# Six changes of order in a two-layer hybrid encoder on one core: low parts, turned pairs, dot products and the sums of its branches

## The chip, the cores and the metric

The kernel runs on one core of one Trainium2 chip. A core has five engines that run at the same time, each through its own queue in order: TensorE (PE, matrix products; its weight loads are PEld), VectorE (DVE), ScalarE (ACT), GpSimd (POOL) and SyncE (SP, which issues DMA transfers). The metric is the device time of one execution in microseconds (us). The time before is 2328.27 us, the median of three runs (2327.64 to 2328.99).

## The reference

The inputs are x (512 tokens by 1024 channels) and one conditioning row c. Each of two layers adds a half-step feed-forward, a mixer of three branches, and another half-step feed-forward; each takes a normed x, scaled and shifted from c:

```python
mod = (c_act @ w_ada[l] + b_ada[l]).reshape(B, N_MOD, D_MODEL)          # nine rows of 1024
h = modulate(rms_norm(x, norm_gain[l, 0]), mod[:, 0], mod[:, 1])
x = x + 0.5 * mod[:, 2][:, None, :] * swiglu(h, ffn_w_gate[l, 0], ffn_w_up[l, 0], ffn_w_down[l, 0])
h = modulate(rms_norm(x, norm_gain[l, 1]), mod[:, 3], mod[:, 4])
x = x + mod[:, 5][:, None, :] * hybrid_mixer(h, ...)
# hybrid_mixer:
proj = h @ w_in
qa, ka, va, ub, qc, kc, vc, f_lin, g_lin = jnp.split(proj, SPLIT_POINTS, axis=-1)
ya = chunked_relpos_attention(...)      # branch A: 8 heads of 64, learned bias by distance
yb = multiscale_pool(ub, ...)           # branch B: window averages of 2, 4, 8, 16 tokens, per group of 128
yc = forgetting_attention(...)          # branch C: causal, forget gates in the logits
branch = jnp.einsum('bsnw,nwd->bsnd', jnp.stack([ya, yb, yc], axis=2), w_branch)
merged = jnp.sum(jax.nn.sigmoid(g_lin.reshape(B, S, 3, D_MODEL)) * branch, axis=2)
return merged @ w_out
```

All is float32. Queries and keys of A and C are RMS-normed per head.

## The kernel before, in words

**Products.** An fp32 operand is cut in a rounded high part (fp32r) and a low part, the rest. A product is three matmuls: high by high, high by low, low by high. `triple` does that for 512 columns (L140 to L142), `add_product` for 256 (L149 to L151); both call `poll` first. High parts are casts on ScalarE (L317 for weights), low parts are subtractions on VectorE (L319), in the first phase on GpSimd. The long products with h (gate and up of the feed-forwards, the gates of the merge) go by a seven-product scheme on blocks: `Seven` makes the weights' sums and splits (L563 to L580, casts L567 and low parts L568), `Blocks` the sums and splits of h, beginning with `h`, which adds high and low part back to full blocks (L522).

**Phases of a layer.** Feed-forward, mixer, feed-forward. The first feed-forward begins with `start`: squares of x, their sum over channels by matmuls with ones (L829), 1/rms by three Newton steps on VectorE (L328 to L337), spread over the partitions by a matmul (L843), and then for each of eight blocks of 128 channels: the weights' chunk (its low part on GpSimd, L319), h scaled (L852), its high part (ScalarE, L854) and low part (VectorE, L857), and 18 matmuls.

The mixer: `proj_qk` and `proj_v` make queries, keys and values of A (columns 0, 1, 2). `proj` evacuates an accumulator per token block; for values that is a cast (L944) and a subtraction (L945) into the tile xv. Then follow attention A with the projections of C (columns 3, 4, 5) as filler between its steps, attention C with the first gate and branch A's merge as filler, the pooling inputs, two tiles of the merge of C (`merge_units`), and the merges by pairs of tiles (`merge_pairs`: three pairs of branch C, four of branch B), then w_out. In attention, L1108 and L1109 are logits, L1112 adds the bias and takes the maximum, L1116 is the exponential, L1120 the division, L1132 turns the probabilities, L1136 and L1137 split them (tiles pta and ptb), and L1154 and L1155 multiply by the values. In `merge_pairs` the sums of branches are `put_c`: gate times branch on VectorE (L1395), then added to the running sum on GpSimd (L1396). `put_b` calls it too, and splits an earlier sum (L1402, L1403).

**Queries and keys** are normed and scaled per token block (`scale`, L980), then turned, 128 channels (a pair of heads) at a time: `turn`, four transposes (L985), a high part on ScalarE (L994) and a low part on VectorE (L1000). There are four PSUM buffers for such results (`mmt`), four accumulators (`acc`), and two buffers of the kind ptb.

**Rows of w_ada.** The 144 blocks of modulation are dot products of VectorE (L227) with rows loaded by DMA (L220). `side_work`, called by each chunk of weights (`wchunk`), loads the next row and computes those loaded, as long as `in_ffn` is set; it is cleared behind the values of A. In the pairs rows are loaded and computed where `rows` is called.

**What sets the order.** `pe[0]` counts TensorE's work in matmuls of 512 columns. `later(delay, fn)` puts a step off until so much work has been issued, and `poll` runs what is due. Queries and keys are normed from such due times, and `ready` turns pair p when due, and not before attention has come to a given head (`heads`). `after` and `behind` put an instruction behind another one in the queue (`tc.issue_after`). The instructions are then laid in each engine's queue by a scheduler; each engine runs its queue in that order and waits on semaphores.

Of the kernel before, what the change touches and what calls it, by code (L numbers as in the profile page):

```python
# [15 lines left out]
F32 = mybir.dt.float32  # L16
# [3 lines left out]
ALU = mybir.AluOpType  # L20
# [20 lines left out]
def encoder_kernel(tc, xT, c, w_ada, b_ada, gains, w_gate, w_up, w_down, w_qkv, w_f, w_ubg,  # L41
# [457 lines left out]
    class Blocks:  # L499
# [18 lines left out]
        def h(self, q):  # L518
            if self.xa is None:
                self.full[q] = blk("v2", F32)  # L520
                k = slice(2 * q, 2 * q + 2)
                nc.vector.tensor_tensor(self.full[q], hhi[:, k, :].bitcast(F32), hlo[:, k, :].bitcast(F32), op=ALU.add)  # L522
# [182 lines left out]
    class Ffn:  # L705
# [112 lines left out]
        def start(self):  # L818
# [15 lines left out]
            r = rsqrt(v, NT)  # L834
            dg = st([P, NT, P], F32, "ssum", 1)
# [5 lines left out]
            spread = gate["vector"]  # L841
# [8 lines left out]
            def h(d):  # L850
                t = t1(T)
                scaled = nc.vector.tensor_tensor(t, rb, xd(d), op=ALU.mult).ins  # L852
                a, b = apre[:, l, 0, d:d + 1], modc[:, l, 0, d:d + 1]
                nc.scalar.activation(hhi[:, d, :], t, AF.Identity, scale=a, bias=b)  # L854
                tb = mmt()
                nc.scalar.activation(tb, t, AF.Identity, scale=a, bias=b)
                nc.vector.tensor_tensor(hlo[:, d, :], tb, hhi[:, d, :].bitcast(F32), op=ALU.subtract)  # L857
# [13 lines left out]
            for d in range(KD):  # L871
                if d == 0:
                    gate["vector"] = spread
# [10 lines left out]
    def qkv_chunk(l, col, c, **kw):  # L884
        return wchunk(w_qkv[l, 2 * c * P:(2 * c + 2) * P, col * T:(col + 1) * T]
                      .rearrange("(k p) c -> p k c", p=P), (2, T), **kw)

    def proj(l, col, evac, pre=None, norm=None):
# [25 lines left out]
        else:  # L914
            for c in range(2):
                if col == 3 and c == 1:
                    gate["vector"] = last["values"]
                hi, lo = qkv_chunk(l, col, c)
# [7 lines left out]
        for t in range(NT):  # L926
            for c, hi, lo in held:
# [8 lines left out]
    def proj_v(l, col, tag, res):  # L936
        vt = [None] * NT

        def evac(t, a):
            b = st([P, H, 2, HD], F32R, tag, 4)  # L940
            a3 = a.rearrange("p (h d) -> p h d", h=H)
            for odd in range(2):
                hi, lo = b[:, odd::2, odd, :], b[:, odd::2, 1 - odd, :]
                nc.scalar.copy(hi, a3[:, odd::2, :])  # L944
# [6 lines left out]
    def proj_qk(l, col, gcol, is_q, res, pre=None, norm=None):  # L951
# [30 lines left out]
        def turn(p):  # L982
# [7 lines left out]
            first, second = slice(0, HD), slice(HD, P)  # L990
            for odd, (own, other) in enumerate(((first, second), (second, first))):
# [288 lines left out]
    def merge_pairs(l, jobs, first, blocks):  # L1280
# [7 lines left out]
        for q, (n, d, ys, put, early, late, behind) in enumerate(jobs):  # L1288
# [38 lines left out]
            tens(c[:, 0], w, c[:, 0], ALU.add)  # L1327
            step("pair34")
# [20 lines left out]
    class Mixer:  # L1349
# [10 lines left out]
        def run(self, nxt):  # L1360
# [31 lines left out]
            def put_c(d, pb, th):  # L1392
# [3 lines left out]
                nc.gpsimd.tensor_tensor(md, md, tmp, op=ALU.add)  # L1396
# [41 lines left out]
            front(3)()  # L1438
            for n, _ in enumerate(merge_units(l, 2, yc, put_c, 2)):
                if n == 4:  # L1440
# [7 lines left out]
                elif n == 14:  # L1448
# [3 lines left out]
            jobs = [(2, 2, yc, put_c, [], [back(3), back(2)], [front(1)]),  # L1452
                    (2, 4, yc, put_c, [cast(1)], [back(1)], [front(0)]),
                    (2, 6, yc, put_c, [cast(0)], [back(0)], [])]
            def rows(*tags):
                def go():
                    mod_flush()
# [5 lines left out]
            def reload():  # L1463
                silc[0] = st([P, D], F32, "b", NB)
                nc.sync.dma_start(silc[0], sil_dram.broadcast_to([P, D]))
                rows("pta", "b")()

            jobs += [(1, d, yb, put_b, [] if d else [reload], [], [rows("pta") if d else rows("pta", "b")]) for d in (0, 2, 4, 6)]
# [93 lines left out]
```

## Time and profile before

| what | us |
|---|---|
| median of three runs | 2328.27 (2327.64 to 2328.99) |
| the profiled execution | 2328.61 |
| its span, first to last instruction | 2326.8 |
| TensorE busy | 2299.0 (99%) |
| VectorE busy | 1855.7 (80%) |
| ScalarE busy | 1240.8 (53%) |
| GpSimd busy | 333.1 (14%) |

TensorE's granted clock is 1.00. Spans and starts in the rows of the profile are microseconds from the first instruction. A row of the timeline is: start, duration, engine, line, operation, written tile <- read tiles, shape, count, and in brackets the engine's idle time before it and what ended it. A row of the list of waits is: the waiting engine and line, what released it, microseconds in total, times, the longest. A row of the windows has the stretch, its length, and the busy time of PE, PEld, DVE, ACT and POOL with their counts, the granted clock, the DMA share and GB/s. Matmuls are pipelined, so that a row's duration (0.39) is longer than the distance of two starts.

### The profile page before, as it was taken

To read this page: it belongs to the slowest core of one execution; us is meant where nothing else is said; L and a number is where in the kernel's file an instruction comes from. 1 tells how busy PE (TensorE), PEld (TensorE's weight loads), DVE (VectorE), ACT (ScalarE), POOL (GpSimd) and SP (SyncE) were. 2 spreads that over 40 slices of the span, in tenths; PEclk is the share of its full clock that TensorE was granted. 3 is DMA by queue.
4 is the path that set the end of the run, shared out by engine and by line. 5 is a ranking of instruction groups with operands and counts; after the bars stand their busy time and mean duration, and the time that the engine had idled before them with its cause. 6 is when DMAs were issued, how large, how long until landed. Compare 5 with 4: busy or idle time off the path is not lost.

```text
span 2326.8 us, 38930 instructions
## 1 busy us (share of the span) xinstructions
PE 2299.0 (99%) x14826; PEld 2067.4 (89%) x14826; DVE 1855.7 (80%) x3172; ACT 1240.8 (53%) x2252; POOL 333.1 (14%) x447
## 2 busy tenths in 40 slices
PE   7999999999999999999999999999999999999999
PEld 5899998778889898989999989988788898999898
DVE  8988877787698778888788989687877986879593
ACT  5353554677654464635553636466765544636362
POOL 3000011244412210000000000122443122000000
PEclk9999999999999999999999999999999999999999
DMA  8736343433234625363426373443333346153322
GB/s 283 252 110 225 120 162 122 120 91 118 96 118 135 204 71 203 101 248 115 145 82 208 91 254 100 163 145 101 94 118 94 118 145 199 55 181 96 114 92 100
DMA packets 142174, 325.26 MB, mean 140 GB/s; under 512 B 14338, under 2 KB 16514, under 8 KB 141988
## 3 DMA queue, kind: packets, MB, share of 16 engines
q1 hardware_dynamic: 137282, 307.05, 40.3%
q0 software_dynamic: 4704, 15.73, 2.2%
q8 instruction: 116, 1.90, 0.3%
q14 instruction: 70, 0.57, 0.1%
q10 hardware_dynamic: 2, 0.00, 0.0%
HBM read 312.16 MB, written 6.38 MB: 137 GB/s over the span
## 4 chain that ended last, share of the span: by engine, by line
PE 87%; DVE 8%; ACT 2%; issue 2%; DMA 1%; SPq 0%; DVEq 0%; ACTq 0%
PE acc L140 12%; PE acc L142 12%; PE acc L141 12%; PE acc L149 6%; PE acc L151 6%; PE acc L150 6%; PE mm L151 5%; PE mm L149 5%; PE mm L150 5%; PE mm L140 4%; PE mm L141 4%; PE mm L142 4%; PE mm L1132 1%; DVE v L227 1%; DVE w L319 1%
## 5 line engine op out<-in xcount | busy, mean ns | idle before, releaser
L317 ACT CAST w<-raw 128x1024 fp32r<-128x1024 f32 (+1 forms) x213 | 219.4, 1040 | 216.4 <-PE acc L142 132.7
L140 PE MATMUL acc<-b,w 128*128 128x512 f32 (+1 forms) x880 | 326.6, 371 | 0.0
L141 PE MATMUL acc<-b,w 128*128 128x512 f32 (+1 forms) x880 | 323.2, 367 | 0.0
L142 PE MATMUL acc<-b,w 128*128 128x512 f32 (+1 forms) x880 | 323.1, 367 | 0.0
L319 DVE TENSOR_TENSOR w<-raw,w 128x1024 fp32r<-128x1024 f32 x205 | 251.2, 1235 | 89.3 <-ACT w L317 85.8
L142 PEld LDWEIGHTS acc<-b,w 128*128 128x128 f32 x880 | 165.3, 188 | 28.1
L140 PEld LDWEIGHTS acc<-b,w 128*128 128x128 f32 x880 | 165.3, 188 | 26.3
L141 PEld LDWEIGHTS acc<-b,w 128*128 128x128 f32 x880 | 165.4, 188 | 25.9
L149 PE MATMUL acc<-b,ptb 128*128 128x256 f32 x588 | 162.9, 277 | 0.0
L150 PE MATMUL acc<-b,ptb 128*128 128x256 f32 x588 | 162.7, 277 | 0.0
L151 PE MATMUL acc<-b,ptb 128*128 128x256 f32 x588 | 162.6, 277 | 0.0
L227 DVE CUSTOM_DVE_ANT_0 v<-v,b,badac 128x1024 f32<-128x1024 f32 x108 | 142.1, 1328 | 5.2 <-DMA v<-in_w_ada_dram 5.2
L140 PE MATMUL acc<-w,hhi 128*128 128x512 f32 x336 | 138.5, 413 | 0.8 <-DVE xv L945 0.7
L141 PE MATMUL acc<-w,hhi 128*128 128x512 f32 x336 | 131.7, 392 | 0.0
L142 PE MATMUL acc<-w,hlo 128*128 128x512 f32 x336 | 131.4, 392 | 0.0
L568 DVE TENSOR_TENSOR ptb<-pta,ptb 128x1024 fp32r<-128x1024 f32 x70 | 85.7, 1224 | 50.9 <-ACT ptb L567 49.8
L149 PE MATMUL mm<-b,ptb 128*128 128x256 f32 x420 | 115.9, 276 | 0.0
L151 PE MATMUL mm<-b,ptb 128*128 128x256 f32 x420 | 115.9, 276 | 0.0
L150 PE MATMUL mm<-b,ptb 128*128 128x256 f32 x420 | 115.9, 276 | 0.0
L568 DVE TENSOR_TENSOR w<-v,w 128x1024 fp32r<-128x1024 f32 x84 | 102.5, 1220 | 16.1 <-ACT w L567 16.1
L478 DVE SCALAR_TENSOR_TENSOR xv<-acc,badac,xv 128x512 f32<-128x512 f32 (+1 forms) x112 | 76.9, 689 | 47.3 <-PE acc L142 47.2
L567 ACT CAST ptb<-raw 128x1024 fp32r<-128x1024 f32 x84 | 88.5, 1053 | 48.4 <-DVE raw L577 48.2
(330 smaller groups left out, 7401.3 us busy)
## 6 DMA issues: line engine op xcount, KB each, us to landing
v<-in_w_ada_dram SPq DMA_DIRECT2D x108, 512.0 KB, 5.5
raw<-in_w_down_dram SPq DMA_DIRECT2D x88, 512.0 KB, 4.2
raw<-in_w_qkv_dram SPq DMA_DIRECT2D x42, 512.0 KB, 3.7
v<-in_w_gate_dram SPq DMA_DIRECT2D x70, 256.0 KB, 4.3
v<-in_w_up_dram SPq DMA_DIRECT2D x70, 256.0 KB, 3.3
raw<-in_w_gate_dram SPq DMA_DIRECT2D x70, 256.0 KB, 3.5
raw<-in_w_up_dram SPq DMA_DIRECT2D x70, 256.0 KB, 3.5
raw<-in_w_ubg_dram SPq DMA_DIRECT2D x28, 512.0 KB, 3.6
```

What stands on the lines that cost most here:

```text
L140: mm(o, lh, rh, start=start, stop=False)
L141: mm(o, lh, rl, start=False, stop=False)
L142: mm(o, ll, rh, start=False, stop=stop)
L149: mm(o, lh, rh, start=start and k == 0, stop=False, skip_group_check=True)
L150: mm(o, lh, rl, start=False, stop=False, skip_group_check=True)
L151: mm(o, ll, rh, start=False, stop=k == 3, skip_group_check=True)
L227: product = lambda: nc.vector.tensor_tensor_reduce(out=raw, in0=raw, in1=silc[0], scale=1.0, scalar=badac[:, l, j, d:d + 1], op0=ALU.mult, ...
L317: nc.scalar.copy(hi, raw)
L319: lo_eng.tensor_tensor(lo, raw, hi.bitcast(F32), op=ALU.subtract)
L478: nc.vector.scalar_tensor_tensor(x, acc_j, gate, x, op0=ALU.mult, op1=ALU.add)
L567: act_(lambda: nc.scalar.copy(pair[0], src))
L568: vec_(lambda: nc.vector.tensor_tensor(pair[1], src, pair[0].bitcast(F32), op=ALU.subtract))
```

## The change

Six things change; no arithmetic does.

1. In `start`, the low part of the weights' first chunk on GpSimd is put behind a small new GpSimd operation (`paused`) that reads 1/rms; before it stood behind the sum of squares.
2. `Blocks.h` (L522 before) is put behind the last low part of h in `start`, as the dots already are where `last["norm"]` is set.
3. The first chunk of column 3 (queries of C) is loaded and split ahead of the last token block of column 2 (values of A), and the casts of its second chunk are put behind the last cast of the values.
4. A pair is turned only when 24 units have been issued since the turn before (`APART`), while attention runs, and keys are due 12 units later.
5. The sums of the pooling's widest window (`front(3)`) are issued behind the first matmuls of the merge of C instead of ahead of them.
6. In the pairs, the running sum is added on VectorE, and the dots of w_ada rows are spread: one at the end of a pair, one in its middle.

```diff
             if self.xa is None:
                 self.full[q] = blk("v2", F32)
                 k = slice(2 * q, 2 * q + 2)
-                nc.vector.tensor_tensor(self.full[q], hhi[:, k, :].bitcast(F32), hlo[:, k, :].bitcast(F32), op=ALU.add)
+                with after("norm"):
+                    nc.vector.tensor_tensor(self.full[q], hhi[:, k, :].bitcast(F32), hlo[:, k, :].bitcast(F32),
+                                            op=ALU.add)
...
             r = rsqrt(v, NT)
+            paused = nc.gpsimd.tensor_scalar(st([P, 16], F32, "hd", 1)[:, :NT], r, 1.0, None, op0=ALU.mult).ins
...
-            spread = gate["vector"]
...
-                nc.vector.tensor_tensor(hlo[:, d, :], tb, hhi[:, d, :].bitcast(F32), op=ALU.subtract)
+                low = nc.vector.tensor_tensor(hlo[:, d, :], tb, hhi[:, d, :].bitcast(F32), op=ALU.subtract)
+                if d == KD - 1:
+                    last["norm"] = low.ins
...
                 if d == 0:
-                    gate["vector"] = spread
+                    gate["vector"] = paused
                 w = wchunk(w_first[d], (6, P), side=False, lo_eng=nc.gpsimd)
...
+    ahead = []
...
                 if col == 3 and c == 1:
-                    gate["vector"] = last["values"]
-                hi, lo = qkv_chunk(l, col, c)
+                    gate["scalar"], gate["vector"] = last["values cast"], last["values"]
+                hi, lo = ahead.pop() if ahead else qkv_chunk(l, col, c)
...
         for t in range(NT):
+            if col == 2 and t == NT - 1:
+                ahead.append(qkv_chunk(l, 3, 0))
             for c, hi, lo in held:
...
+            turned[0] = pe[0]
             for odd, (own, other) in enumerate(((first, second), (second, first))):
...
-                if heads[0] < (Q_GATE if is_q else K_GATE)[p]:
+                if heads[0] < (Q_GATE if is_q else K_GATE)[p] or (heads[0] < H and pe[0] < turned[0] + APART):
                     later(8, lambda: ready(p))
...
-            later(TURN + 12 * p, lambda p=p: ready(p))
+            later(TURN + (0 if is_q else 12) + 12 * p, lambda p=p: ready(p))
...
-    TURN = 52
+    turned = [0.0]
+    TURN, APART = 52, 24
...
             tens(c[:, 0], w, c[:, 0], ALU.add)
+            for fn in middle:
+                fn()
             step("pair34")
...
                 vec_(lambda: nc.vector.scalar_tensor_tensor(tmp, th, 1.0, pb, op0=ALU.add, op1=ALU.mult))
-                nc.gpsimd.tensor_tensor(md, md, tmp, op=ALU.add)
+                vec_(lambda: nc.vector.tensor_tensor(md, md, tmp, op=ALU.add))
...
-            front(3)()
             for n, _ in enumerate(merge_units(l, 2, yc, put_c, 2)):
-                if n == 4:
+                if n == 0:
+                    front(3)()
+                elif n == 4:
...
-            jobs += [(1, d, yb, put_b, [] if d else [reload], [], [rows("pta") if d else rows("pta", "b")]) for d in (0, 2, 4, 6)]
+            jobs += [(1, 0, yb, put_b, [reload], [], [], [rows(2, "b", "pta")]),
+                     (1, 2, yb, put_b, [], [rows(1)], [], [rows(1, "pta")]),
+                     (1, 4, yb, put_b, [], [rows(1, "pta")], [], []),
+                     (1, 6, yb, put_b, [], [rows(1, "pta")], [], [])]
```

How the queues change is seen at three places. The line numbers of the changed kernel are larger by 2 to 12: L985 is L993 there, L1108 is L1118, L1132 is L1142, L1154 is L1164.

TensorE in attention A, layer 0, where the second pair of C's queries is turned (mm is a PSUM tile, ident,ptb a turn of queries, ident,t a turn of probabilities, acc<-w the projection that fills in). Before:

```order
L1108 MATMUL mm_5071<-b_4399,b_4145 128x512
L1109 MATMUL mm_5071<-b_4399,b_4146 128x512
L985 MATMUL mm_5083<-ident,ptb_4705 128x128 x4
L140 MATMUL acc_4859<-w_4997,hhi 128x512
L141 MATMUL acc_4859<-w_4997,hhi 128x512
L1132 MATMUL mm_5098<-ident,t_826_4986 128x128 x2
```

In the changed kernel, from the same logits on:

```order
L1118 MATMUL mm_5076<-b_4418,b_4147 128x512
L1119 MATMUL mm_5076<-b_4418,b_4148 128x512
L1142 MATMUL mm_5088<-ident,t_828_4991 128x128 x2
L140 MATMUL acc_4864<-w_5002,hhi 128x512
L141 MATMUL acc_4864<-w_5002,hhi 128x512
```

The turn L985 is gone from behind the logits; it now stands 23 rows further down the queue, with two groups of turned probabilities, a product by the values and another pair of logits in between.

VectorE behind the keys of A, layer 0 (nt_q, nt_u, nt_z are Newton steps, L980 scales the four token blocks of ptb, L319 is the low part of the last chunk of A's values). Before:

```order
L336 SCALAR_TENSOR_TENSOR nt_u_4300<-nt_q_4299,nt_v_633_4237 128x32
L337 SCALAR_TENSOR_TENSOR nt_z_4301<-nt_u_4300,nt_z_4259 128x32
L980 TENSOR_TENSOR ptb_4131<-ptb_4131,nt_z_4301 128x512 x2
L1052 TENSOR_SCALAR t_642_4272<-t_642_4272 8x512
L980 TENSOR_TENSOR ptb_4131<-ptb_4131,nt_z_4301 128x512 x2
L1054 SCALAR_TENSOR_TENSOR t_641_4269<-t_641_4269,t_642_4272 8x512
L319 TENSOR_TENSOR w_4391<-raw_4389,w_4391 128x1024
L1056 SCALAR_TENSOR_TENSOR t_643_4278<-t_641_4269 8x512
```

In the changed kernel (L988 is the scaling, L1062, L1064, L1066 and L1072 are L1052, L1054, L1056 and L1062 before):

```order
L227 ISA pta_4479,badac<-pta_4479,b_73,badac 128x1024
L227 ISA badac 128x1
L335 TENSOR_TENSOR nt_q_4301<-nt_z_4261 128x32
L336 SCALAR_TENSOR_TENSOR nt_u_4302<-nt_q_4301,nt_v_634_4239 128x32
L337 SCALAR_TENSOR_TENSOR nt_z_4303<-nt_u_4302,nt_z_4261 128x32
L1062 TENSOR_SCALAR t_643_4274<-t_643_4274 8x512
L988 TENSOR_TENSOR ptb_4133<-ptb_4133,nt_z_4303 128x512 x2
L1064 SCALAR_TENSOR_TENSOR t_642_4271<-t_642_4271,t_643_4274 8x512
L988 TENSOR_TENSOR ptb_4133<-ptb_4133,nt_z_4303 128x512
L1066 SCALAR_TENSOR_TENSOR t_644_4280<-t_642_4271 8x512
L988 TENSOR_TENSOR ptb_4133<-ptb_4133,nt_z_4303 128x512
L1072 TENSOR_SCALAR strip_4282<-t_644_4280 8x128
```

A dot product L227 (with the read of its sum) stands ahead of the last Newton step, the four scalings are spread over the forget gate's steps, and the low part L319, ahead of the scan before, comes behind the scan and the four strips L1072 now, four rows below the last one shown, with that of the next chunk behind it.

VectorE at the end of `start` (hlo is the low part of h, L522 the sum of a block). Before:

```order
L857 TENSOR_TENSOR hlo<-mm_395,hhi 128x512
L227 ISA v_75_401,badac<-v_75_401,b_73,badac 128x1024
L227 ISA badac 128x1
L522 TENSOR_TENSOR v_97_539<-hhi,hlo 128x1024
L227 ISA v_80_452,badac<-v_80_452,b_73,badac 128x1024
L227 ISA badac 128x1
L857 TENSOR_TENSOR hlo<-mm_431,hhi 128x512
```

In the changed kernel:

```order
L859 TENSOR_TENSOR hlo<-mm_397,hhi 128x512
L227 ISA v_76_403,badac<-v_76_403,b_73,badac 128x1024
L227 ISA badac 128x1
L859 TENSOR_TENSOR hlo<-mm_433,hhi 128x512
L227 ISA v_81_454,badac<-v_81_454,b_73,badac 128x1024
```

The block sum has left its place; between the last two low parts of h stands one dot.

More of the change, by code (lines that the diff above doesn't have):

```diff
@@ L943, in evac @@
                 hi, lo = b[:, odd::2, odd, :], b[:, odd::2, 1 - odd, :]
-                nc.scalar.copy(hi, a3[:, odd::2, :])
+                last["values cast"] = nc.scalar.copy(hi, a3[:, odd::2, :]).ins
                 last["values"] = nc.vector.tensor_tensor(lo, a3[:, odd::2, :], hi.bitcast(F32), op=ALU.subtract).ins
@@ L1287, in merge_pairs @@
         todo = [first, Seven(gates(*jobs[1][:2]), ENTRY, stag="v2")]
-        for q, (n, d, ys, put, early, late, behind) in enumerate(jobs):
+        for q, (n, d, ys, put, early, middle, late, behind) in enumerate(jobs):
             now = todo.pop(0)
@@ L1450, in run, with rows @@
             first.second()
[L1452 to L1455, printed above, removed]
+            jobs = [(2, 2, yc, put_c, [], [], [back(3), back(2)], [front(1)]),
+                    (2, 4, yc, put_c, [cast(1)], [], [back(1)], [front(0)]),
+                    (2, 6, yc, put_c, [cast(0)], [], [back(0)], [])]
+            def rows(dots, *tags):
                 def go():
-                    mod_flush()
+                    mod_flush(len(loaded) - dots)
                     for tag in tags:
```

2 lines of the change are left out of this document (1 added, 1 removed).

## The prediction

> **What bounds the kernel now.** I read the page first, then the list of TensorE's waits, then the timeline around each wait that the change touches.
>
> ```profile
> span 2326.8 us, 38930 instructions
> PE 2299.0 (99%) x14826; PEld 2067.4 (89%) x14826; DVE 1855.7 (80%) x3172; ACT 1240.8 (53%) x2252; POOL 333.1 (14%) x447
> ```
>
> TensorE is busy for 99% of the span and the change removes no matmul. Only what TensorE loses between matmuls can be won, and the list of waits says how much that is (line, what it waited for, sum in us, times, longest):
>
> ```profile
> PE mm L843 <- ACT ssum L838: 4.5, 1, 4.5
> ...
> PE mm L1132 <- DVE b L1000: 2.4, 2, 1.2
> PE acc L149 <- ACT v L1286: 1.6, 2, 0.8
> PE mm L985 <- DVE mx L1112: 1.5, 2, 0.8
> PE acc L141 <- DVE hlo L857: 1.4, 1, 1.4
> PE acc L142 <- DVE w L319: 0.9, 2, 0.5
> PE mm L1155 <- DVE ptb L1137: 0.7, 2, 0.4
> PE acc L140 <- DVE xv L945: 0.7, 1, 0.7
> ...
> PE mm L985 <- DVE pta L1137: 0.5, 2, 0.2
> ```
>
> All the rows from L1132 down lie at places that the diff rewrites: 2.4 + 1.6 + 1.5 + 1.4 + 0.9 + 0.7 + 0.7 + 0.5 = 9.7 us in both layers. That is nearly the ceiling of the gain, to which the start (L843) could add. A wait with "2, 1.2" occurs once in each layer. Against these few us stand the prices: every edit moves work on VectorE, which is nearly full at just these places.
>
> **The change part by part.** 1. *The low part of the last h ahead of the block sum* (first feed-forward).
>
> ```profile
> 50.69 2.87 DVE L522 TENSOR_TENSOR v<-hhi,hlo 128x1024 f32<-128x1024 f32 x1
> 53.48 1.27 DVE L227 CUSTOM_DVE_ANT_0 v<-v,b,badac 128x1024 f32<-128x1024 f32 x1
> 54.68 0.68 DVE L857 TENSOR_TENSOR hlo<-mm,hhi 128x512 fp32r<-128x512 f32 x1
> 55.42 0.50 PE L141 MATMUL acc<-hlo,w 128*128 128x512 f32 x1 [1.37 <-DVE hlo L857]
> ```
>
> VectorE spends 50.69 to 54.68 on a block sum and a dot product before L857 makes the low part that TensorE waits for. Now only a dot of 1.27 us stands there, so L857 ends before 53.5, and TensorE needs it 1.37 us before 55.42, at 54.05. The wait goes: **-1.4**. The block sums come later and nothing reads them before the first seven-product stretch.
>
> 2. *The first low part of the weights waits for 1/rms* (GpSimd, L319).
>
> ```profile
> 13.79 1.80 POOL L319 TENSOR_TENSOR w<-raw,w 128x768 fp32r<-128x768 f32 x1 [12.47 <-ACT w L317]
> 13.93 1.68 DVE L335 TENSOR_TENSOR nt_q<-nt_j 128x4 f32<-128x4 f32 x1
> 16.03 0.16 DVE L335 TENSOR_TENSOR nt_q<-nt_z 128x4 f32<-128x4 f32 x1
> 17.01 0.16 DVE L337 SCALAR_TENSOR_TENSOR nt_z<-nt_u,nt_z 128x4 f32<-128x4 f32 x1
> 17.68 1.28 DVE L227 CUSTOM_DVE_ANT_0 v<-v,b,badac 128x1024 f32<-128x1024 f32 x1
> 20.19 1.80 POOL L319 TENSOR_TENSOR w<-raw,w 128x768 fp32r<-128x768 f32 x1 [4.60 <-DVE badac L227]
> 20.76 2.31 DVE L227 CUSTOM_DVE_ANT_0 v<-v,b,badac 128x1024 f32<-128x1024 f32 x1
> ```
>
> The first L335 took 1.68 us instead of 0.16 and ended with GpSimd's subtraction (15.61 against 15.59). This lies on the chain to 1/rms, behind which TensorE waits 4.5 us. With the subtraction moved, 1/rms (17.01 + 0.16) is there 1.5 us earlier, at 15.7. But GpSimd then starts it at about 15.9, behind a small operation of its own, and VectorE's next large work is the dot that now starts at 17.68, and would start at about 16.2. The second pair of rows shows what follows: a dot begun 0.57 us behind GpSimd's start takes 2.31 instead of 1.28 and ends 1.08 after it. So the moved dot would end at 15.9 + 1.80 + 1.08 = 18.8, where it ends now (17.68 + 1.28, less the overlap of its accumulator read, 18.89). The first h waits behind the dots: **0**. If the dot is first, the gain is 1.4, and I keep -1.4 to +0.5 for the range.
>
> This price hangs on one rule of the Trainium skill ("SBUF — State Buffer", section "Who interferes with whom"): a VectorE instruction with two SBUF inputs and a GpSimd instruction that reads SBUF lock each other out, and issue order decides who waits. The rule would speak against this edit, since the dot has two such inputs as L335 has, and the trace agrees with both pairs above (1.68 against 0.16, 2.31 against 1.28). By the rule it is 0 if GpSimd comes first and -1.4 if the dot does.
>
> 3. *The first chunk of the queries of C is cast ahead of the last token block of A's values.* Its low part no longer stands between the last value parts and TensorE: the wait on xv L945 goes, **-0.7**. But its loader is now called while the phase still loads rows of w_ada with every chunk, so each layer gets one row more on SP's queue here and a dot more on VectorE, in the middle of the steps that norm the keys of A (the second order fence of the section on the change).
>
> ```profile
> 421.59 0.19 DVE L337 SCALAR_TENSOR_TENSOR nt_z<-nt_u,nt_z 128x32 f32<-128x32 f32 x1
> 424.04 1.27 DVE L980 TENSOR_TENSOR ptb<-ptb,nt_z 128x512 f32<-128x512 f32 x2
> 424.82 0.88 PE L985 MATMUL mm<-ident,ptb 128*128 128x128 f32 x4
> 425.25 0.67 DVE L1054 SCALAR_TENSOR_TENSOR t<-t,t 8x512 f32<-8x512 f32 x1
> 425.85 1.21 DVE L319 TENSOR_TENSOR w<-raw,w 128x1024 fp32r<-128x1024 f32 x1
> 426.98 1.21 DVE L1056 TENSOR_TENSOR_SCAN t<-t 8x512 f32<-8x512 f32 x1
> 428.23 0.87 DVE L1062 TENSOR_SCALAR strip<-t 8x128 f32<-8x128 f32 x3
> 429.02 0.47 DVE L1062 TENSOR_SCALAR ssum<-t 8x512 f32<-8x512 f32 x1
> 430.12 0.40 PE L140 MATMUL acc<-w,hhi 128*128 128x512 f32 x1
> 430.36 0.39 PE L141 MATMUL acc<-w,hhi 128*128 128x512 f32 x1
> ```
>
> The row is sent behind the chunk before, and I take it as landed. The dot costs 1.2 between two starts. Behind it stand the rest of the last norm step (three like L337, 0.2 each), an operation on 8 partitions (0.4, as the last L1062), two scalings (1.2), L1054 (0.6), a scaling (0.6), the scan (1.2), the last scaling (0.6): 421.8 + 1.2 + 0.6 + 0.4 + 1.2 + 0.6 + 0.6 + 1.2 + 0.6 = 428.2, where the four scalings were done by 425.3 (424.04 + 1.27). The turn is 12 matmuls later than at 424.82, at 0.23 each (430.12 to 430.36) at 427.6, and its last transpose would start at 427.9: 0.4 late. Then four strips (1.25) and the low part of the last values' chunk (1.21) end at 430.7; TensorE wants it eight matmuls behind the turn, at about 430.1: another 0.7. That is 1.1 in each layer, **+2.2**; between 0 (the dot falls into a gap) and +4.
>
> 4. *Turned pairs further apart.* The second turn of C's queries used the last of four PSUM buffers of its kind, since b L1000 of the first turn had not been read out; in the new order (first order fence) attention's work stands between them. The 2.4 and the 0.5 (pta L1137) go: **-2.9**. The keys' first turn (1.5 behind mx L1112, held up by four scalings in a row) keeps its four scalings in a row, with a low part of 1.2 now ahead of them, but has more of attention's matmuls before the turn; 0 to -1.5, and I take half, **-0.75**. The 0.7 at L1155 has VectorE's crowding alone as cause; half, **-0.35**. The price: the fourth turn of the queries, later now, reads the last of a tile of which there are only two buffers (ptb), and attention's next probabilities are cast into that buffer. TensorE has some ten matmuls (2.2 us) between that turn and the product that reads them, and the two casts, of four and of three blocks, at most 0.6 each:
>
> ```profile
> 482.40 0.58 ACT L1136 CAST ptb<-mm 128x512 fp32r<-128x512 f32 x1
> ```
>
> The exponentials queued behind these casts on ScalarE come later too. Bounds 0 and 2 in each layer; as the slack is about as long as the casts I take 0.4 each, **+0.8**.
>
> 5. *The pooling's first sums behind the gate's first chunk.* The two waits on w L319 (0.9) had a pooling sum of VectorE ahead of the low part: **-0.9**.
>
> 6. *Branch pairs: sums on VectorE, a dot in mid-pair.*
>
> ```profile
> 760.90 1.60 POOL L1396 TENSOR_TENSOR xv<-xv,t 128x512 f32<-128x512 f32 x1 [10.67 <-DVE t L1395]
> 761.28 2.31 DVE L227 CUSTOM_DVE_ANT_0 pta<-pta,b,badac 128x1024 f32<-128x1024 f32 x1
> 765.33 0.68 DVE L1403 TENSOR_TENSOR b<-xv,b 128x512 fp32r<-128x512 f32 x1
> 765.93 1.78 DVE L571 TENSOR_TENSOR raw<-raw,v 128x512 f32<-128x512 f32 x1
> 675.00:800.00 125.00, 124.20 (x833) 114.12 (x832) 107.64 (x125) 62.33 (x109) 30.74 (x24) 1.00 0.45 146
> ```
>
> Twice here a VectorE operation is held by GpSimd's sum, by 1.03 (a dot, 2.31 against 1.28) and 1.1 (L571, 1.78 against 0.68 for L1403 of the same size). With a second dot between them this makes L577 late, and behind it ScalarE's cast, its copy L1286, and a product that waits 0.8 for that copy. A sum on VectorE costs 0.6 (765.33 to 765.93) and holds nobody; two of them add 1.2, two holds less win 2.1, and the moved dot wins 1.2. L577 comes about 2 us earlier: the wait goes, **-1.6**. VectorE is busy 107.6 of 125 us in this stage; 14 sums add 8.4, less the holds.
>
> The first matmul behind a wait takes 0.50 (L141 at 55.42) instead of 0.39 (at 430.36): ten waits less, **-1.0**. The sum: -1.4 - 0.7 + 2.2 - 2.9 - 0.75 - 0.35 + 0.8 - 0.9 - 1.6 - 1.0 = **-6.6**. The profiled execution took 2328.61 (span 2326.8 and 1.8 around it), 0.3 above the median of 2328.27; against the median I forecast **2321.7 us**. Likeliest range of its own: 2318.5 to 2324.5.
>
> **The rivals.** *A, the new queues take the gain back.* The two-buffer tile costs 2 in each layer (+3.2 on my sum), and the dots that the later block sums push behind them reach the first seven-product stretch, which loads into the buffers that they free (+1.4, all that the start won). 2321.7 + 4.6 = 2326.3; 2324.9 with the first alone. For it: VectorE is nearly full there; against it: the turns have more room.
>
> *B, the start gains as well.* The dot is first at the start (-1.4), the keys' turn has no wait (-0.75), the row of w_ada falls into gaps (-2.2): 2317.3. For it: 1/rms is 1.5 earlier beyond doubt; against it: GpSimd's start at 15.9 is ahead of the dot's by 0.3.
>
> *C, slower: VectorE becomes the bound of the pairs.* If GpSimd's sums do not hold VectorE elsewhere in the stage, each of the 14 pairs has 1.2 us more on it, in front of L571 and L577. It decides where a pair's chain has no slack left, as in the one at 765. If all 14 lose 1.2, 16.8 us; less the 1.6 no longer won, 2321.7 + 16.8 + 1.6 = 2340. Against it: even with all sums added and no hold gone, 116 of 125 us are busy.
>
> *D, the change does little.* The spaced turns only move their waits (+2.9 and +1.1) and the sums in pairs only exchange holds for work (+1.6): 2327.3.
>
> **How the numbers follow.** The forecast 0.45, A 0.25, B 0.15, D 0.09, C 0.06. A measurement can tell 0.2% from no change, 4.7 us: faster is below 2323.6, slower above 2332.9. Faster: nearly all of B and most of the forecast's own range, 0.15 + 0.42, and a little of A where its prices are smaller, 0.04: 0.61. Slower: C and a stray case, 0.07. The rest, 0.32, within 0.2%. The range of eight in ten takes in B and A, and the upper ends of D: 2316 to 2328.
>
> **What would show it.** No wait of L141 for the last hlo near 54, and a first L335 of 0.16 with a dot of 2.3 behind it: steps 1 and 2. If that dot takes 1.28, B is right on it. A wait of TensorE at the first turn of A's keys and one at the chunk behind it, a dot among the norm's steps: step 3. No L1132 wait on a turned low part, and L1154 waiting, or not, for ptb cast behind the fourth turn: step 4 and A. In the pairs no L571 of 1.78, no wait of L149, VectorE busier: step 6; new waits at every pair: C. I am wrong if waits appear at places where the diff changes nothing, or if the sum of TensorE's waits falls as forecast and the time does not.

## The result, and the profile after

The changed kernel takes 2347.55 us (median of 6 runs, 2346.42 to 2348.5), the kernel before 2328.07 (median of 6 too): the ratio is 1.0083, with a 95% interval of 1.007 to 1.0096. It is 19.5 us slower, where 2321.7 was forecast with a range of 2316 to 2328.

TensorE's waits, on which the whole forecast was built, went down. The list of waits of the changed kernel (line, releaser, sum, times, longest), without the three waits of the start:

```profile
PE mm L1142 <- POOL t L1130: 2.6, 2, 1.3
PE acc L140 <- ACT hhi L856: 1.8, 1, 1.8
PE mm L1165 <- DVE ptb L1147: 1.1, 2, 0.6
PE acc L141 <- DVE hlo L859: 1.1, 1, 1.1
PE mm L1165 <- DVE pta L1147: 1.0, 2, 0.5
PE mm L1142 <- DVE pta L1147: 0.6, 2, 0.3
PE mm L993 <- DVE ptb L988: 0.6, 2, 0.3
PE acc L141 <- DVE w L319: 0.4, 2, 0.2
PE mm L388 <- DVE strip L376: 0.3, 1, 0.3
```

Of the waits that the prediction counted, those of 2.4, 1.6, 1.5, 0.9 and 0.5 and the 0.7 on xv are gone. The other 0.7, on ptb (L1155, now L1165), is 1.1, and others, of 2.6 and 1.0, are new. Behind the start the rows of the list come to 9.5 us, where they were 11.9 (with 1.7 for the first h and 0.5 at L1154, which the prediction's list leaves out). Yet the span is 18.2 us longer, and the page shows on which engine:

```profile
span 2345.0 us, 38887 instructions
PE 2319.4 (99%) x14826; PEld 2088.3 (89%) x14826; DVE 1851.1 (79%) x3204; ACT 1247.7 (53%) x2252; POOL 279.8 (12%) x416
```

TensorE is busy for 2319.4 us, where it was 2299.0 with the same 14826 matmuls. So it does not wait longer, it works longer. A window in the first feed-forward, in which TensorE never stands still, shows the rate: before, then after (the first figures are the length and PE's busy time and count).

```profile
130.00:330.00 200.00, 200.00 (x1532) 190.95 (x1531) 173.81 (x255) 105.54 (x181) 0.00 (x0) 1.00 0.46 150
```

```profile
130.00:330.00 200.00, 200.00 (x1508) 191.46 (x1507) 170.26 (x252) 104.64 (x180) 0.00 (x0) 1.00 0.44 148
```

1532 matmuls in 200 us became 1508, at a granted clock of 1.00 both times, with VectorE less busy and GpSimd idle. Three groups of the changed kernel tell which matmuls these are, with the same groups of the kernel before behind them (busy time in us, mean ns of one):

```profile
L141 PE MATMUL acc<-b,w 128*128 128x512 f32 x704 | 274.3, 390 | 0.0
L149 PE MATMUL acc<-b,ptb 128*128 128x256 f32 x588 | 165.4, 281 | 0.0
L149 PE MATMUL mm<-b,ptb 128*128 128x256 f32 x420 | 118.0, 281 | 0.0
```

```profile
L141 PE MATMUL acc<-b,w 128*128 128x512 f32 x704 | 274.3, 390 | 0.0
L149 PE MATMUL acc<-b,ptb 128*128 128x256 f32 x588 | 162.9, 277 | 0.0
L149 PE MATMUL mm<-b,ptb 128*128 128x256 f32 x420 | 115.9, 276 | 0.0
```

Where the weights lie in w and the product has 512 columns nothing changed. Where they lie in ptb, each of the seven-product scheme's matmuls takes 4 to 6 ns more. There are twelve such groups (L149 to L151; acc and mm; b, and hhi or hlo, streamed), 4032 matmuls; their busy times together grow by 19.1 us, which is most of the loss. The scheme's other matmuls, whose weights lie in w, grow by 2.2 in all, those of L150 with b streamed by 2 to 3 ns each (before, then after):

```profile
L150 PE MATMUL mm<-b,w 128*128 128x256 f32 x140 | 38.6, 276 | 0.0
```

```profile
L150 PE MATMUL mm<-b,w 128*128 128x256 f32 x140 | 39.0, 278 | 0.0
```

The 256-column products of `triple` with weights in ptb grow by 0.8. That makes 22.1 us of longer matmuls; the waits, shorter by 2.4, take a part back.

What these products have in common with the change is not the order. The small tile into which GpSimd now copies 1/rms has the kind `hd`. A kind gets its place when it is first used; `hd` was first used in the pooling, as the last of all, and is now first used in `start`. All kinds first used later lie 64 bytes further. The places in the two built programs (bytes from the start of each partition):

```text
kind                 before     after
hhi, hlo             18688, 35072       the same
b (17 tiles)         51456 and on       the same
w (3)                121088 and on      the same
raw (2)              182048     182112
t1, t2               190240     190304
pta                  200480     200544
ptb (2)              204608     204672
strip (2)            221056     221120
hd                   229056     182048
```

hhi, hlo, b and w begin on multiples of 128, and so does ptb now; before, ptb began 64 behind one. These are the tiles: the scheme's weights in w begin 64 or 32 bytes into theirs (`place` in `duo`), so they did not begin on a multiple of 128 either.

### The profile page after: what moved, and what is told of

The parts are those of the page before. It is cut to its first block, busy times and chain, and to the rows that moved or that the text cites. A ratio compares the mean times of both kernels' runs of the same rounds, so it can differ in the third digit from the quotient of the medians.

```text
span 2345.0 us, 38887 instructions
## 1 busy us (share of the span) xinstructions
PE 2319.4 (99%) x14826; PEld 2088.3 (89%) x14826; DVE 1851.1 (79%) x3204; ACT 1247.7 (53%) x2252; POOL 279.8 (12%) x416
## 4 chain that ended last, share of the span: by engine, by line
PE 90%; DVE 6%; ACT 2%; DMA 1%; issue 1%; SPq 0%; POOL 0%; DVEq 0%; ACTq 0%; POOLq 0%
PE acc L140 12%; PE acc L142 12%; PE acc L141 12%; PE acc L149 7%; PE acc L150 7%; PE acc L151 7%; PE mm L150 5%; PE mm L149 5%; PE mm L151 5%; PE mm L141 5%; PE mm L140 5%; PE mm L142 5%; PE mm L1142 1%; DMA pta<-in_w_ada_dram 1%; DVE w L319 1%
## 5 line engine op out<-in xcount | busy, mean ns | idle before, releaser
L319 DVE TENSOR_TENSOR w<-raw,w 128x1024 fp32r<-128x1024 f32 x205 | 249.7, 1228 | 80.8 <-ACT w L317 80.4
L150 PE MATMUL acc<-b,ptb 128*128 128x256 f32 x588 | 165.6, 282 | 0.0
L149 PE MATMUL acc<-b,ptb 128*128 128x256 f32 x588 | 165.4, 281 | 0.0
L151 PE MATMUL acc<-b,ptb 128*128 128x256 f32 x588 | 164.8, 280 | 0.0
L227 DVE CUSTOM_DVE_ANT_0 v<-v,b,badac 128x1024 f32<-128x1024 f32 x106 | 139.4, 1329 | 5.8 <-DMA v<-in_w_ada_dram 5.6
L150 PE MATMUL mm<-b,ptb 128*128 128x256 f32 x420 | 118.4, 282 | 0.0
L149 PE MATMUL mm<-b,ptb 128*128 128x256 f32 x420 | 118.0, 281 | 0.0
L151 PE MATMUL mm<-b,ptb 128*128 128x256 f32 x420 | 117.6, 280 | 0.0
L570 DVE TENSOR_TENSOR ptb<-raw,ptb 128x1024 fp32r<-128x1024 f32 x84 | 102.6, 1221 | 12.3 <-ACT ptb L569 12.3
```

The source lines that it names most:

```text
L149: mm(o, lh, rh, start=start and k == 0, stop=False, skip_group_check=True)
L150: mm(o, lh, rl, start=False, stop=False, skip_group_check=True)
L151: mm(o, ll, rh, start=False, stop=k == 3, skip_group_check=True)
L227: product = lambda: nc.vector.tensor_tensor_reduce(out=raw, in0=raw, in1=silc[0], scale=1.0, scalar=badac[:, l, j, d:d + 1], op0=ALU.mult, ...
L319: lo_eng.tensor_tensor(lo, raw, hi.bitcast(F32), op=ALU.subtract)
L570: vec_(lambda: nc.vector.tensor_tensor(pair[1], src, pair[0].bitcast(F32), op=ALU.subtract))
```

## The experiments

In two theories the 19.5 us come from the *place of tiles*, or from the new *order* of VectorE, ScalarE and GpSimd, which would slow the products by contention. The first four kernels tell them apart.

**e1: the copy of 1/rms goes into a kind of tile that exists already.** Every tile then lies where it lay before; the order of all queues is that of the change.

```diff
-            paused = nc.gpsimd.tensor_scalar(st([P, 16], F32, "hd", 1)[:, :NT], r, 1.0, None, op0=ALU.mult).ins
+            paused = nc.gpsimd.tensor_scalar(st([P, NT], F32, "nt_q", 1), r, 1.0, None, op0=ALU.mult).ins
```

> The changed kernel, with the copy of 1/rms by GpSimd written into the tile kind nt_q, which exists already, so that no tile moves: in the changed kernel the 64 bytes of hd stand ahead of raw, t, pta, ptb and strip, which all lie 64 bytes further. Theory 'place of tiles' (products whose stationary weights lie in ptb run at 116 to 120 ns instead of 112 because ptb moved by 64 bytes): the pace goes back to 112 and some 18 us with it, to about 2329 us, in which the waits won and lost remain. Theory 'order' (the new order of VectorE, ScalarE and GpSimd slows the products by contention): the pace stays at 116 to 120 and the time at 2347.

Measured: 2325.56 us, ratio to the kernel before 0.9989 (0.9979 to 0.9998). The group is back at its old time:

```profile
L149 PE MATMUL acc<-b,ptb 128*128 128x256 f32 x588 | 162.8, 277 | 0.0
```

2347.55 - 2325.56 = 22.0 us hang on one line that computes nothing, where some 18 were expected: the expectation had counted the scheme's products with weights in ptb alone, and not the 2.2 and 0.8 of the others. The order theory falls; what the six edits do otherwise is a gain of 2.6 us (2328.12 before in this set).

**e2: ptb alone 64 bytes further, in the kernel before.** The unused pad ahead of ptb takes over the 64 bytes of the one behind it. No instruction changes. (The source has one line fewer, so L149 is L148.)

```diff
-            st([P, 8], F32, "pad", 1)
+            st([P, 24], F32, "pad", 1)
             t, place = st([P, 4 * T], F32R, tag, 2), 0
-            st([P, 16], F32, "pad2", 1)
```

> The kernel before with the unused pad ahead of ptb made 64 bytes larger and the one behind it left out: ptb alone lies 64 bytes further, no instruction changes. Place of tiles: the products with stationary weights in ptb slow from 112 to 116 to 120 ns, 4032 of them by some 4.6 ns, 18.5 us: about 2346. Order: nothing changes, 2328.

Measured: 2349.68, ratio 1.0093 (1.0078 to 1.0108): 21.6 us slower, by ptb's place alone.

```profile
L148 PE MATMUL acc<-b,ptb 128*128 128x256 f32 x588 | 165.5, 281 | 0.0
```

**e3: raw, t1, t2, pta, ptb and strip 128 bytes further, in the kernel before.**

```diff
+            st([P, 32], F32, "pad3", 1)
             dg = st([P, NT, P], F32, "ssum", 1)
```

> The kernel before with 128 unused bytes where the changed kernel has its 64: raw, t, pta, ptb, strip all lie 128 bytes further. Place of tiles, in the form that the place within 128 bytes counts (hhi, hlo, b and w begin on multiples of 128, ptb at 64 behind one before the change, on one after it): as before, 2328. If any move of ptb or of the others costs, or the distance to something else: slower, toward 2346. Order: 2328.

Measured: 2332.58, ratio 1.0018 (1.0009 to 1.0027). Twice the way costs 4.5 us and not 21.6: it is not how far a tile is moved that counts, but it is not the place within 128 bytes alone either.

**e4: ptb alone 32 bytes further.** The pads have 16 and 8 words.

```diff
-            st([P, 8], F32, "pad", 1)
+            st([P, 16], F32, "pad", 1)
             t, place = st([P, 4 * T], F32R, tag, 2), 0
-            st([P, 16], F32, "pad2", 1)
+            st([P, 8], F32, "pad2", 1)
```

> The kernel before with ptb alone 32 bytes further (96 behind a multiple of 128). Place of tiles, within 128 bytes: something between, 2328 to 2346, slower than 2328 if a distance of 32 from the moving operands' places is already bad; within 64 bytes (if only an even or odd multiple of 64 counts): 2328. Order: 2328.

Measured: 2353.85, ratio 1.011 (1.0094 to 1.0127), the slowest of all, outside what was expected of a place in between.

```profile
L149 PE MATMUL acc<-b,ptb 128*128 128x256 f32 x588 | 166.1, 283 | 0.0
```

Three more kernels asked what place means. **f1: every operand of the products 64 bytes further.**

```diff
+    cp.tile([P, 16], F32, name="padc")
     hhi = cp.tile([P, KD, T], F32R, name="hhi")
```

> The kernel before with 64 unused bytes ahead of hhi: every operand of the products lies 64 bytes further, ptb and what streams past it keep their distance. Theory 'distance' (the place of the weights relative to the streamed operand counts): as before, 2328. Theory 'absolute place' (weights that begin on a multiple of 128 are slow, at 64 behind one fast): ptb's products slow as in e2, and those with weights in w, which now begin at 64 behind one, may gain: 2340 to 2350 or some way below.

Measured: 2328.76 against 2328.49, ratio 1.0 (0.999 to 1.0009). ptb lies at 204672 as in the slow kernel, and is fast:

```profile
L149 PE MATMUL acc<-b,ptb 128*128 128x256 f32 x588 | 162.8, 277 | 0.0
```

So it is the distance between the weights and the other operands of the product that counts, not the place itself.

**f2: ptb 128 bytes further, the strips and small tiles behind it 64, in the kernel before.**

```diff
-            st([P, 8], F32, "pad", 1)
+            st([P, 40], F32, "pad", 1)
             t, place = st([P, 4 * T], F32R, tag, 2), 0
-            st([P, 16], F32, "pad2", 1)
```

> The kernel before with ptb 128 bytes further and the strips and small tiles behind it 64. If the place within 128 bytes is all that counts: 2328. In the run with all tiles behind the small ones 128 further, ptb's products lost 2.3 and 0.9 ns each; if that was ptb's own place, 2332 here too; if it was raw, t or pta, 2328.

Measured: 2332.83, ratio 1.0019 (1.001 to 1.0029), as e3: the 4.5 us at 128 bytes are ptb's own.

**f3: the pads of e2 in the changed kernel.** ptb then lies 128 bytes behind its first place; raw, t1, t2, pta and strip stay where the change put them.

> The changed kernel with ptb another 64 bytes further, so that it begins again at 64 behind a multiple of 128; raw, t, pta and strip stay where the change put them. If ptb alone cost the 22 us between e1 and the changed kernel: 2326 to 2330. If raw, t and pta have their share: between 2330 and 2347.

Measured: 2331.56, ratio 1.0014 (1.0005 to 1.0024). That is 16.0 us faster than the changed kernel, and 6.0 above e1, some 4.3 to 4.5 of it by f2 and e3 for ptb's 128 bytes. Little is left for the other moved tiles.

The remaining kernels take e1, in which no tile moves, and undo one part each.

**e5: turned pairs as before.** `APART` 0, and no 12 units for the keys.

```diff
-    TURN, APART = 52, 24
+    TURN, APART = 52, 0
...
-            later(TURN + (0 if is_q else 12) + 12 * p, lambda p=p: ready(p))
+            later(TURN + 12 * p, lambda p=p: ready(p))
```

> The changed kernel with no tile moved (as e1), and the turned pairs of queries and keys as before (no distance of 24 units, keys not 12 later). Theory 'two buffers' (the later turns make the keys' normed tile wait for a buffer of ptb, ScalarE waits 2.4 us in its queue, and GpSimd's division comes 1.3 late): the waits L1142 behind GpSimd and L1165 go and those of before (L1132 on b L1000, L985 on mx) come back; from 475 to 575 us of each layer 10.7 us above pace become 10.1, 1.3 faster in all than e1, about 2324.3. Prediction's step 4: 2.2 to 3.2 slower, about 2328.

Measured: 2330.34, ratio 1.0013 (1.0004 to 1.0022), 4.8 slower than e1. The theory of the two buffers seemed to fall. Its list of waits shows a place that neither theory had named:

```profile
PE mm L993 <- DVE ptb L988: 4.5, 6, 1.4
...
PE mm L1142 <- DVE b L1009: 2.4, 2, 1.2
PE mm L993 <- DVE mx L1122: 1.6, 2, 0.8
```

Some 4.0 of the 4.5 us (2.3 in the first layer, 1.7 in the second) are waits at the turns of A's keys: without the 12 units these meet the dot of the extra row of w_ada. The others are the old ones of attention A.

**e6: e1 without the extra row.** The chunk that is loaded ahead is loaded with `side=False`.

```diff
-                ahead.append(qkv_chunk(l, 3, 0))
+                ahead.append(qkv_chunk(l, 3, 0, side=False))
```

> As e1, but the chunk that is loaded ahead loads no row of w_ada with it, so that no dot stands among the norm's steps of the keys of A. Theory 'extra row' (prediction's step 3): the two waits at the first turn and at the low part behind it, 0.48 + 0.37 us and their restarts in each layer, go: 2.2 faster than e1, about 2323.3. Rival (VectorE is late there anyway, since the low part of the next chunk stands there now): less than 0.5, about 2325.3.

Measured: 2324.89, ratio 0.9985 (0.9976 to 0.9994). The waits in question, in e1 and then here:

```profile
PE mm L993 <- DVE ptb L988: 1.0, 3, 0.5
PE mm L1165 <- DVE pta L1147: 1.0, 2, 0.5
PE acc L141 <- DVE w L319: 0.7, 2, 0.4
```

```profile
PE acc L141 <- DVE hlo L859: 0.9, 1, 0.9
...
PE mm L993 <- DVE ptb L988: 0.5, 2, 0.3
```

The wait on w L319 is gone and half of that on L988. In e1 they stood at A's keys: two in the first layer, as below, and one of 0.36 on w L319 in the second, 1.2 in all.

```profile
427.62 0.33 PE L993 MATMUL mm<-ident,ptb 128*128 128x128 f32 x1 [0.48 <-DVE ptb L988]
...
429.93 0.50 PE L141 MATMUL acc<-w,hhi 128*128 128x512 f32 x1 [0.37 <-DVE w L319]
```

The medians differ by 0.7 and not by 2.2, and the two intervals overlap: what the row costs is not settled between nothing and 2 us. Another wait, on hlo L859 near 42 in the start, is 0.2 in e1 and 0.9 here with no edit there. It costs nothing: the product behind it starts 19.78 us behind the first product of the feed-forward in both (42.02 - 22.24 and 41.69 - 21.91).

**b1 and b2: e6 with the turns as before, and with the keys' 12 units but no distance.**

```diff
# b1, on e6
-    TURN, APART = 52, 24
+    TURN, APART = 52, 0
...
-            later(TURN + (0 if is_q else 12) + 12 * p, lambda p=p: ready(p))
+            later(TURN + 12 * p, lambda p=p: ready(p))
# b2, on e6: the first of the two alone
```

> No tile moved, no extra row (as e6), and all turns of queries and keys as before. Theory 'two buffers' (distance costs in attention A because the keys' normed tile of C waits for a buffer of ptb; and the 4.8 us of e5 came from A's keys, turned early into the extra row's dot): without the extra row the old turns cost nothing at A's keys, and in attention A they have 13.1 us above pace from 450 to 600 against 13.9 in e6, in each layer: 1 to 1.7 faster than e6, about 2323.5. Theory 'distance wins' (prediction's step 4): 2 to 5 slower than e6, 2327 to 2330.

> As e6, keys due 12 units later as in the changed kernel, but no distance between turns (queries of C as before). Tells the two halves of the turns' change apart: if the distance costs, 1 to 1.7 faster than e6 and like b1 (2323.5); if the distance wins, 2 to 5 slower than e6.

Measured: b1 2323.39, ratio 0.9979 (0.997 to 0.9987); b2 2323.72, 0.9982 (0.9973 to 0.9991). Without the extra row the old turns are 1.5 and 1.2 faster than the new ones, as the theory of the two buffers had it; the intervals overlap, and the profiled executions do not show it (spans of 2321.9 in e6 and 2322.0 in b1), so the sign is likely and the size is not known. What is excluded is that the old turns cost the 2 to 5 us that step 4 gave them. The extra row also explains e5: with the old turns the extra row costs 2330.34 - 2323.39 = 7.0 us, with the later ones 0.7. So the later turns protected the extra row of the same change. That it is the 12 units of the keys is argued and not shown by a run of its own: the distance holds only while attention runs, and these turns come before it.

What the distance brings stands in e1's timeline, ScalarE first, then GpSimd and TensorE:

```profile
498.69 1.08 ACT L967 COPY ptb<-acc 128x512 f32<-128x512 f32 x2 [2.44 <-PE mm L1165]
...
501.39 1.48 POOL L1130 TENSOR_SCALAR t<-t,rs 128x384 f32<-128x384 f32 x1 [0.71 <-DVE rs L1128]
...
502.93 0.33 PE L1142 MATMUL mm<-ident,t 128*128 128x128 f32 x1 [1.30 <-POOL t L1130]
```

C's queries keep one of the two ptb tiles until their fourth turn, attention's probabilities have the other, and the copy of the first normed keys must wait for the product that reads them. ScalarE stands 2.44 us in its queue; the exponential behind the copy, the division and the turn of the probabilities are late by as much as TensorE waits, 1.30.

**b3: a distance of 14 in place of 24, on e6; b5: the same without the pause of e8.**

```diff
-    TURN, APART = 52, 24
+    TURN, APART = 52, 14
```

> As e6, with a distance of 14 units in place of 24: the four turns of C's queries stand evenly, and the fourth where it stood before, so that the keys' tile finds its buffer. Theory 'two buffers': the wait behind b L1000 is gone and those behind GpSimd's division (1.3) and on ptb (0.6) do not come: some 2 to 3 faster in each layer than e6, 2319 to 2321. Theory 'crowding' (the waits of e1 come from VectorE's and ScalarE's order and not from the buffer): as e6, 2324.9.

> As the kernel with a distance of 14, and without the pause of the first low part (as e8). If the lock has only moved: as that kernel or up to 0.5 faster. If the pause wins 1.5: 1.5 slower.

Measured: b3 2325.47, ratio 0.9989 (0.998 to 0.9998); b5 2325.43, 0.999 (0.9981 to 0.9999). 2319 to 2321 was expected of b3, and missed. The waits behind GpSimd and behind b L1009 are both gone from its list, but there is a new one:

```profile
PE mm L1118 <- DVE ptb L1147: 5.4, 6, 1.2
```

Logits wait for a PSUM buffer that VectorE has not read out. In this stretch the wait goes where the slack was; no distance tried beats the old turns.

**e7: e1 with the running sums on GpSimd again.**

```diff
-                vec_(lambda: nc.vector.tensor_tensor(md, md, tmp, op=ALU.add))
+                nc.gpsimd.tensor_tensor(md, md, tmp, op=ALU.add)
```

> As e1, with the running sums of the pairs on GpSimd again, the dots in mid-pair kept. Theory 'holds' (GpSimd's sums hold VectorE's two-input operations, 1.0 to 1.1 us each): the wait of 0.8 behind ScalarE's copy at the second pair of branch B comes back in each layer, about 1.8 slower than e1, 2327.4. Rival (the moved dot alone removed that wait): no change, 2325.6.

Measured: 2324.98, ratio 0.9986 (0.9976 to 0.9995), no slower than e1. The holds are there as before, GpSimd's two sums and a VectorE operation held by each:

```profile
759.42 1.61 POOL L1408 TENSOR_TENSOR xv<-xv,t 128x512 f32<-128x512 f32 x1 [10.66 <-DVE t L1407]
759.80 2.32 DVE L227 CUSTOM_DVE_ANT_0 pta<-pta,b,badac 128x1024 f32<-128x1024 f32 x1
...
763.01 1.47 POOL L1408 TENSOR_TENSOR xv<-xv,t 128x512 f32<-128x512 f32 x1
763.25 1.78 DVE L573 TENSOR_TENSOR raw<-raw,v 128x512 f32<-128x512 f32 x1
```

but no product waits at a pair. The dots' new places were enough by themselves to remove that wait. (The medians alone, 0.6 apart, would not exclude the 1.8 expected; the list of waits does.)

**e8: e1 without the pause of the first low part.**

```diff
-            paused = nc.gpsimd.tensor_scalar(st([P, NT], F32, "nt_q", 1), r, 1.0, None, op0=ALU.mult).ins
...
+            spread = gate["vector"]
...
-                    gate["vector"] = paused
+                    gate["vector"] = spread
```

> As e1, without the small operation that makes the first low part wait for 1/rms. Theory 'the lock moved' (GpSimd's subtraction now holds the two operations that spread 1/rms, 2.08 us instead of 0.48, as it held the first Newton step before): no change or up to 0.5 faster, 2325.1 to 2325.6. Rival (the pause wins the 1.5 us of the Newton step and something else loses it): 1.5 slower, about 2327.1.

Measured: 2325.35, ratio 0.9987 (0.9978 to 0.9996), as e1. The pause wins nothing, and e1's timeline shows why:

```profile
14.35 0.16 DVE L335 TENSOR_TENSOR nt_q<-nt_j 128x4 f32<-128x4 f32 x1
...
16.19 2.08 DVE L843 TENSOR_SCALAR ssum<-ident,nt_z 128x128 f32<-128x128 f32 x2
```

```profile
16.39 1.79 POOL L319 TENSOR_TENSOR w<-raw,w 128x768 fp32r<-128x768 f32 x1
```

The Newton step takes 0.16 again, and the two operations that spread 1/rms now take 2.08, held by the same subtraction. In the kernel before they took 0.48:

```profile
17.28 0.48 DVE L840 TENSOR_SCALAR ssum<-ident,nt_z 128x128 f32<-128x128 f32 x2
```

With `spread`, as in the kernel before, the subtraction is put behind the operations that spread 1/rms, and not behind the sum of squares. That is an order and no wait: in e8 it starts at 13.41 and they at 17.11, and a step of the Newton iteration is held again (L328, 1.62 in place of 0.17).

## Why the prediction was wrong, step by step

**The premise failed.** The first part said that the change removes no matmul and that "only what TensorE loses between matmuls can be won". A matmul's own time was taken as fixed. It is not: 22.0 us of the result (2347.55 against e1's 2325.56) are longer matmuls: 4032 that run 4 to 6 ns slower because their weights lie 64 bytes further, and others, shown above, that make up some 3 us of it. The edit that does it was named in step 2, as "a small operation of its own", and its tile was priced at nothing. The kernel before even shows the care: two unused pads stand around ptb. No rival had it either; the slower one, C, put 2340 down to VectorE in the pairs, where nothing went wrong. The prediction's last sign of being wrong, that the waits fall and the time does not, is what came: the waits fell by 2.4 of the 5.6 counted, and the time rose.

**What is left, the order, was -2.6 (e1) where the sum said -6.6.**

- *Step 1* (-1.4): right. The wait behind the block sum at 54 is gone, and from the first product to the first seven-product matmul TensorE takes 101.5 us in e1 where it took 102.9. The wait on the low part of another h near 42 (1.1 in the changed kernel, 0.2 in e1) costs nothing, as e6 shows.
- *Step 2* (0, the lock moves with GpSimd's subtraction): right in size by e8. The place was wrong: not the dot but the two operations that spread 1/rms are held. So the dot of 1.28, which the prediction would have read as a sign for rival B, came (1.27 in e1) without B's gain. The Trainium skill ("SBUF — State Buffer", section "Who interferes with whom") counts such an operation with one input among those that can take the shared ports; the trace agrees, with 2.08 against 0.48.
- *Step 3* (-0.7 and +2.2): the wait on xv is gone. The new waits stand where they were put, in the first layer with 0.48 at the first turn (0.4 said) and 0.37 at the low part (0.7 said), in the second with the low part's 0.36 alone: 1.2 in all. By the medians of e1 and e6 their price is 0.7, with an uncertainty as large. That the same row would cost 7.0 with the old turns was not seen.
- *Step 4* (-2.9, -0.75, -0.35, against +0.8): this step failed. The waits on b L1000 and mx L1112 did go, but the price of the two-buffer tile was mis-sized: 0.4 in each layer was said, and TensorE waits 1.3 there behind GpSimd, and 0.5 and 0.6 at L1165, where it was 0.4. The prediction had looked for it at the probabilities' cast behind the fourth turn; it came at the copy of the keys. By the medians the distance costs 1.2 to 1.5 (b1 and b2 against e6), a size that is not known, where the step had a gain of 3.2, which is excluded.
- *Step 5* (-0.9): the two waits on w L319 behind the pooling sums are gone from the list.
- *Step 6* (-1.6): the wait is gone, but the reason was half wrong. The holds by GpSimd are real and cost nothing here (e7); the moved dots did it.
- *The restarts* (-1.0) went with step 4: about as many waits came as went.

The lowest median is that of b1: the change with no tile moved, no extra row and the old turns, 2323.39 us, 0.9979 (0.997 to 0.9987) of the kernel before and 24 us below the change as it was made.

## What to carry to other kernels

Before the waits of a change are counted, compare the places of all tiles in the two built programs: a kind of tile that is first used earlier moves everything allocated behind it. And look at the mean time of each group of matmuls after the change, not only at idle time: a busy engine at 99% can be 1% slower with fewer waits. When several edits are made together, test them with the places held fixed first, since one of them may protect another (the later turns and the extra row), and undoing one alone then tells little.

## What was not expected of the hardware

The rate of back-to-back matmuls depends on where the weights lie relative to the other operands. For 256-column products with weights in ptb the mean was 277 ns at the distance before, 281 at 64 bytes more (e2), 283 at 32 more (e4), 278 at 128 more (f2), and 277 with all operands moved together by 64 (f1). In total that is 21.6, 25.7 and 4.3 us of this kernel, and nothing for f1. From start to start, the scheme's matmuls with weights in ptb are 113.7 ns apart in e1 and 118.3 in the changed kernel. The loss also reaches weights that did not move: of those in w, the first three behind a change from ptb go from 117, 115 and 114 ns to 119, 122 and 119, and from the fourth on there is next to no difference. The rule behind it stays open: 64 and 128 behave differently, so the distance within 128 bytes explains most of it and not all, and which of the operands (the streamed one, or the weights in w ahead and behind) sets it was not tried apart.
